# First MLP group of a streaming encoder layer: blocks 0 and 1 go down by seven quadrant products, ahead of the third block's down, with input sums on VectorE and norm transposes placed later

## The chip, the cores and the metric

The kernel runs on one core of a Trainium2 chip. The core has TensorE (matrix products, into PSUM), VectorE, ScalarE and GpSimd (elementwise work; only the first two reach PSUM) and SyncE, which issues transfers; GpSimd issues transfers as well. Each engine takes its own instructions in order and waits on semaphores for the others. The profile calls them PE, DVE, ACT, POOL and SP.

The metric is the device time of one launch in microseconds. Before the change it is 1217.69 us, the median of three runs (1216.7 to 1219.08).

## The reference

The reference computes one layer of a post-norm encoder for 1024 prompt tokens and 32 tokens of a running stream, both of width 1024:

- h = LN(x) * (1 + scale1) + shift1, with the scales, shifts and gates from a conditioning vector;
- a token mixer (gated linear attention in four heads beside a gated MLP with position mixing), an output projection, and x = LN(alpha * x + (1 + gate1) * (mix W_o + b_o));
- h2 = x * (1 + scale2) + shift2, f = relu(h2 W_up + b_up)^2 W_down + b_down, with W_up 1024 x 4096;
- x = LN(alpha * x + (1 + gate2) * f).

All inputs are float32. The kernel splits each factor into a rounded part and a remainder and adds three products (rounded times rounded, and the two mixed ones), so each logical product is three passes on TensorE.

## The kernel before

The 1056 tokens are columns in three blocks: blocks 0 and 1 of 384 prompt tokens, and block 2 of 256 prompt and 32 stream tokens. Activations lie with features on the partitions. The change is in the last stage, which begins with the output projection of blocks 1 and 2 and holds the first norm's second use (norm1), the MLP in eight groups of 512 hidden features, and the last norm.

**Groups 1 to 7.** Blocks 0 and 1 are the two column halves of one matrix, and each group's weights are cut into four quadrants. Up and down are computed for these two blocks by a Strassen-Winograd scheme: seven quadrant products (P1 to P7) in place of eight, with sums of weight quadrants (`_sums`, L1083 to L1086, on GpSimd) and sums of input quadrants. The sums of the up inputs are the same for all groups; `t_prod` (L1260 on) makes them once, from h2 of blocks 0 and 1, in four steps kk: eight sums on GpSimd (L1271 to L1275), then four splits (L1038 on ScalarE, L1039 on VectorE), each written to DRAM (L1281). From there GpSimd loads them into six ring slots (L1323) for each group. For down, `f_split` makes the sums and splits of the hidden activations F from the group itself (L1337 to L1346). The ring slots lie in the memory of h2 of blocks 0 and 1. Block 2 is always computed the plain way (`up_b2`, `down_b2`, L1236 and L1247).

**Group 0.** The first group is plain for all blocks: four up units (L1226, L1227 split the activation) and four down units, each for three blocks. It runs while norm1 of blocks 1 and 2 and `t_prod` are still at work. Its order is: units 0 and 1 on block 0, then on block 1; then a wait for h2 of block 2; then block 2 of units 0 and 1, and units 2 and 3 on all blocks; then a wait for the end of `t_prod`; then the four down units.

**What sets the order.** TensorE's order is written by a planner (`Order`): streams yield planned costs and delays in nanoseconds, and the one of lowest priority number that is due goes next. `yield 0, 2500` in norm1 is such a delay, ahead of the transposes of y (L1142), and the one at L1188 stands ahead of the transposes that make h2 (L227, read out at L233 on VectorE, L236 on ScalarE and L239 on GpSimd). The other engines' order is set by a scheduler that starts from the order of the text.

**Weights.** `W` loads units of 512 KB into four buffers `raw` (SP, L1095) and splits them into eleven buffers `hl` (three more once the ring exists). A split takes one `hl`, and a load one `raw`; `keep` holds some of both back for `t_prod`: a load goes only with more than `keep[0]` buffers free, a split only with more than `keep[1]`. Loads are issued in a fixed order: output projection, group 0's up units, its down units, then the groups.

## Time and profile before

| What | Value |
|---|---|
| Median of three runs | 1217.69 us |
| Profiled execution, its own time | 1219.88 us |
| Span of its profile | 1218.1 us |
| TensorE busy | 1169.3 us, 96% |
| VectorE, ScalarE, GpSimd busy | 75%, 43%, 39% |
| Last output projection's end to group 1's first products | 483.66 to 632.44 us of the span |
| One steady group | about 83.8 us |

All starts are in microseconds from the start of the span. A group of instructions is named by line, engine, operation, and "out<-in" by the program's names; after the bar stand its busy time, the mean length of one in nanoseconds, and the idle time of the engine ahead of it with what ended it. In a timeline each row is a start, a length and a count, with the idle time before in brackets. In a table of windows each engine's column is its busy time, PEclk the granted clock of TensorE as a share of full speed. The chain of waits goes back from the last instruction: at each step to what released it.

### The profile page before, as it was taken

How to read it: one execution, taken by the hardware profiler on the slowest of the kernel's cores; microseconds unless marked ns; L12 is line 12 of the kernel's file. 1: busy time of each engine (PE TensorE's matmuls, PEld its weight loads, DVE VectorE, ACT ScalarE, POOL GpSimd, SP SyncE). 2: the span in 40 equal slices, each digit the busy share in tenths (PEclk: the TensorE clock that was granted, in tenths of full speed). 3: DMA queues.
4: the chain of work that ended last, by engine and by line, in shares of the span. 5: the costliest groups of instructions: out<-in, count | busy, mean ns of one | idle time of the engine just before them, and what ended most of it. 6: DMA issues, size and time to landing. Idle time of an engine off the chain costs nothing.

```text
span 1218.1 us, 22199 instructions
## 1 busy us (share of the span) xinstructions
PE 1169.3 (96%) x8539; PEld 1114.4 (91%) x8539; DVE 909.8 (75%) x1905; ACT 521.2 (43%) x1065; POOL 469.4 (39%) x682
## 2 busy tenths in 40 slices
PE   5999999999899999899989999999999999999996
PEld 3678999988788999799989999999999999999996
DVE  5664797579896688756759769589499597697577
ACT  4462322446566665642425343343443443433321
POOL 2443110345684154348541442334414414422034
PEclk9999999999899999889989999999999999999998
DMA  9632564110012765204762672743825726737412
GB/s 370 239 126 90 180 214 125 36 36 20 23 37 76 263 219 165 83 31 169 251 242 70 210 252 91 244 171 120 300 100 184 265 70 207 246 100 226 157 73 104
DMA packets 49498, 188.46 MB, mean 155 GB/s; under 512 B 5328, under 2 KB 10928, under 8 KB 49392
## 3 DMA queue, kind: packets, MB, share of 16 engines
q1 hardware_dynamic: 31824, 97.38, 23.4%
q0 software_dynamic: 17568, 89.66, 21.5%
q8 instruction: 67, 1.10, 0.4%
q14 instruction: 39, 0.32, 0.1%
HBM read 171.36 MB, written 15.66 MB: 154 GB/s over the span
## 4 chain that ended last, share of the span: by engine, by line
PE 76%; DVE 11%; DMA 4%; POOL 3%; ACT 2%; issue 2%; SPq 0%; POOLq 0%; DVEq 0%; ACTq 0%
PE mm L250 26%; PE mm L1375 16%; PE mm L1442 12%; PE mm L1236 9%; PE mm L284 3%; PE zp L284 3%; DVE hl L1039 2%; DMA raw<-in_w_dram 2%; DVE acc L1467 1%; DMA wst<-in_w_dram 1%; PE zp L250 1%; DMA tdT<-hl 1%; PE mm L1142 1%; PE gt L783 1%; PE mm L227 1%
## 5 line engine op out<-in xcount | busy, mean ns | idle before, releaser
L1038 ACT CAST hl<-raw 128x512 fp32r<-128x512 f32 (+1 forms) x238 | 143.7, 613 | 242.9 <-PE mm L1442 93.3
L1039 DVE TENSOR_TENSOR hl<-raw,hl 128x512 fp32r<-128x512 f32 (+1 forms) x238 | 203.5, 861 | 40.8 <-ACT hl L1038 40.8
L1375 PE MATMUL mm<-ring,hl 128*128 128x384 f32 x960 | 173.7, 338 | 3.4 <-DMA ring<-tdT 3.4
L1375 PEld LDWEIGHTS mm<-ring,hl 128*128 128x128 f32 x960 | 168.9, 190 | 3.8 <-issue 3.7
L1442 PE MATMUL mm<-ring,hl 128*128 128x384 f32 x792 | 140.8, 335 | 1.3 <-DVE acc L1467 1.3
L1442 PEld LDWEIGHTS mm<-ring,hl 128*128 128x128 f32 x792 | 137.5, 188 | 1.9 <-ACT ring L1038 1.4
L250 PE MATMUL mm<-hT,whl 128*128 128x384 f32 (+1 forms) x792 | 129.0, 322 | 0.0
L250 PEld LDWEIGHTS mm<-hT,whl 128*128 128x128 f32 x792 | 127.0, 188 | 1.1 <-issue 1.1
L250 PE MATMUL mm<-h,hl 128*128 128x288 f32 (+1 forms) x756 | 122.3, 318 | 1.7 <-POOL h L239 1.4
L250 PEld LDWEIGHTS mm<-h,hl 128*128 128x128 f32 x756 | 115.4, 196 | 4.6 <-POOL h L239 3.6
L1083 POOL TENSOR_TENSOR raw<-raw 128x512 f32<-128x512 f32 x26 | 35.9, 1383 | 184.7 <-DMA raw<-in_w_dram 155.3
L1467 DVE SCALAR_TENSOR_TENSOR acc<-mm,G,acc 128x384 f32<-128x384 f32 x162 | 93.7, 607 | 5.4 <-PE mm L1442 4.8
L1236 PE MATMUL mm<-fb,hl 128*128 128x288 f32 x708 | 97.0, 295 | 0.0
L1236 PEld LDWEIGHTS mm<-fb,hl 128*128 128x128 f32 x708 | 95.4, 188 | 0.0
L1247 DVE SCALAR_TENSOR_TENSOR acc<-mm,G,acc 128x256 f32<-128x256 f32 (+3 forms) x176 | 61.8, 390 | 12.0 <-PE mm L1236 11.8
L250 PE MATMUL mm<-mhl,hl 128*128 128x384 f32 (+1 forms) x384 | 65.3, 325 | 2.0 <-ACT hl L1038 1.8
L250 PEld LDWEIGHTS mm<-mhl,hl 128*128 128x128 f32 x384 | 60.3, 192 | 2.6 <-ACT hl L1038 2.1
L1323 POOL DMA_DIRECT2D ring<-tdT x56 | 31.3, 560 | 71.8 <-PE mm L1375 38.2
L284 PE MATMUL zp<-zvw,hT 128*128 128x512 f32 x192 | 52.9, 418 | 4.5 <-ACT hT L236 4.5
L1399 DVE TENSOR_TENSOR tmps<-mm,tmps 128x384 f32<-128x384 f32 x28 | 15.6, 558 | 50.4 <-PE mm L1375 50.4
L1345 ACT CAST ring<-F 128x768 fp32r<-128x768 f32 x42 | 35.1, 837 | 40.0 <-DVE F L1337 20.0
L217 POOL TENSOR_SCALAR rs<-mv 128x1 f32<-128x1 f32 (+1 forms) x27 | 8.6, 322 | 111.1 <-DVE mv L216 108.5
(253 smaller groups left out, 2282.2 us busy)
## 6 DMA issues: line engine op xcount, KB each, us to landing
ring<-tdT POOLq DMA_DIRECT2D x56, 768.0 KB, 5.9
raw<-in_w_dram SPq DMA_DIRECT2D x80, 512.0 KB, 3.9
ring<-tdB POOLq DMA_DIRECT2D x42, 768.0 KB, 6.4
wst<-in_w_dram SPq DMA_DIRECT2D x34, 512.0 KB, 4.4
wad<-in_w_dram POOLq DMA_DIRECT2D x24, 512.0 KB, 4.6
tdT<-hl SPq DMA_DIRECT2D x16, 384.0 KB, 2.9
st<-in_w_dram SPq DMA_DIRECT2D x10, 512.0 KB, 10.2
tdB<-h SPq DMA_DIRECT2D x6, 768.0 KB, 4.4
```

What stands on the lines that cost most here:

```text
L250: PE.matmul(pt[:, :n], h[:, a, 128 * kk:128 * kk + 128], act[:, b_, k, :n], start=(i == 0 and j == 0), stop=(i == 7 and j == 2))
L284: PE.matmul(pt[:n, :width], act[:, a, k, off:off + n], hl[:, b_, width * kk:width * kk + width], start=(k == 0 and a + b_ == 0), stop=(k = ...
L1038: S.copy(hl[:, 0, :n], src)
L1039: V.tensor_tensor(hl[:, 1, :n], src, hl[:, 0, :n].bitcast(F32), ALU.subtract)
L1083: G.tensor_tensor(s, a21, a22, ALU.add)
L1236: PE.matmul(pt[:, :n], hl[kk // 2][:, a, o_:o_ + 128], f(kk)[:, c_], start=(kk == 0 and j == 0), stop=(kk == 3 and j == 2))
L1247: V.scalar_tensor_tensor(ac, pt[:, o + lo - p0:o + hi - p0], G2[:, m, c:c + 1], ac, ALU.mult, ALU.add)
L1323: G.dma_start(s, td[t, j].rearrange("p (a c) -> p a c", a=2))))
L1345: S.copy(q[:, 0], src)
L1375: PE.matmul(pt[:, :384], hl[:, a, o_:o_ + 128], quad(ts[j])[:, b_, kk], start=first and j + kk + i == 0, stop=j + kk + i == 4, skip_group_ ...
L1442: PE.matmul(pt[:, :384], hl[:, a, o_:o_ + 128], f[:, b_, kk], start=first and kk + i == 0, stop=kk + i == 3, skip_group_check=True)
L1467: V.scalar_tensor_tensor(ac, v, G2[:, m, 0:1], ac, ALU.mult, ALU.add)
```

## The change

- Group 0's down weights become a bundle with quadrant sums like those of the later groups, and are loaded only after `t_prod` has taken its two `raw` buffers (`W.open`); `keep` now holds back only `hl`.
- `t_prod` takes its two `raw` buffers once and keeps them for all four steps, its sums move from GpSimd to VectorE, its planned step is 7000 instead of 9000, and its priority is ahead of the main stream.
- Group 0's up runs units 0 and 1 on blocks 0 and 1, then units 2 and 3 on blocks 0 and 1, and block 2 of all four units last. For blocks 0 and 1 the activation stays in float32 (`up_plain`: two ScalarE operations), to be split later by `f_split`.
- Group 0's down for blocks 0 and 1 is by seven quadrant products, ahead of block 2's down. The ring's queue starts with group 0's seven splits of F.
- In norm1 the transposes of y are planned 2500 ns later, and those that make h2 of block 2 another 1500.
- The sums kept for P1 start with group 0 instead of group 1.

```diff
@@ -1044,7 +1044,7 @@
...
         self.loads, self.steps, self.out, self.raw = [], [], {}, {}
-        self.keep = (0, 0)
+        self.keep, self.open = 0, False

@@ -1089,14 +1089,14 @@
...
             go = False
-            if self.loads and len(raws.free) > self.keep[0]:
+            if self.loads and raws.free and (self.open or self.loads[0][0][0] != "d"):
                 key, u = self.loads.pop(0)
...
                 slot, f, k = self.steps[0]
-                if (k is None or k in self.raw) and (len(hls.free) > self.keep[1] if slot else halves.free):
+                if (k is None or k in self.raw) and (len(hls.free) > self.keep if slot else halves.free):
                     self.steps.pop(0)
@@ -1122,11 +1122,10 @@
...
     W.unit(("u", 0, m), U_UP + m)
-for i in range(4):
-    W.unit(("d", 0, i), U_DN + i)
-for g in range(1, 8):
+for g in range(8):
     u, d = U_UP + 4 * g, U_DN + 4 * g
-    W.bundle((("u", g, 0), (u, u + 2)), (("u", g, 1), (u + 1, u + 3)))
+    if g:
+        W.bundle((("u", g, 0), (u, u + 2)), (("u", g, 1), (u + 1, u + 3)))
     if g < 7:
@@ -1172,7 +1171,7 @@
...
     tl = xr[b]
-    yield 0, 2500
+    yield 0, 5000
     for wi, (off, n, _) in enumerate(WIN[b]):
@@ -1185,7 +1184,7 @@
...
             x_rows(b + 1)
-    yield 0, 5500 if b < 2 else 2500
+    yield 0, 5500 if b < 2 else 4000
     h2b = actp.tile([P, 2, KT, BLK[b][1]], F32R, tag=f"act{b}", name=f"h2{b}")
@@ -1228,6 +1227,14 @@
...

+def up_plain(hl, m, b, f):
+
+    def done(pt):
+        t = tmp_tile("rl")
+        S.activation(t, pt[:, :384], AF.Relu, bias=col("b_up", m))
+        S.activation(f, t, AF.Square)
+    yield from fm_tile(hl, h2[b], 384, done)
+
 def down_mm(pt, hl, q, f, n):
@@ -1263,16 +1270,18 @@
...
             DM.dma_start(tv[t, j], h2[b][:, :, k0 + 2 * j:k0 + 2 * j + 2, :].bitcast(F32))
+    yield lambda: len(raws.free) >= 2
+    r = [raws.take() for _ in range(2)]
+    W.open = True
     for kk in range(4):
-        yield lambda: len(raws.free) >= 2 and len(hls.free) >= 2
-        r = [raws.take() for _ in range(2)]
+        yield lambda: len(hls.free) >= 2
         b11, b12, b21, b22 = (r[i][:, 512 * j:512 * j + 384] for i in range(2) for j in range(2))
         for d_, b, k in ((b11, 0, kk), (b12, 1, kk), (b21, 0, kk + 4), (b22, 1, kk + 4)):
-            G.tensor_tensor(d_, h2[b][:, 0, k].bitcast(F32), h2[b][:, 1, k].bitcast(F32), ALU.add)
-        G.tensor_tensor(b11, b12, b11, ALU.subtract)
-        G.tensor_tensor(b12, b22, b12, ALU.subtract)
-        G.tensor_tensor(b22, b22, b11, ALU.subtract)
-        G.tensor_tensor(b21, b21, b22, ALU.subtract)
+            V.tensor_tensor(d_, h2[b][:, 0, k].bitcast(F32), h2[b][:, 1, k].bitcast(F32), ALU.add)
+        V.tensor_tensor(b11, b12, b11, ALU.subtract)
+        V.tensor_tensor(b12, b22, b12, ALU.subtract)
+        V.tensor_tensor(b22, b22, b11, ALU.subtract)
+        V.tensor_tensor(b21, b21, b22, ALU.subtract)
         for t, src in (("T1", b11), ("T3", b12), ("T2", b22), ("T4", b21)):
@@ -1280,10 +1289,10 @@
...
             hls.give(h)
-        for x_ in r:
-            raws.give(x_)
-        yield 0, 9000
-    W.keep = (0, 0)
+        yield 0, 7000
+    for x_ in r:
+        raws.give(x_)
+    W.keep = 0

@@ -1317,7 +1326,7 @@
...
     def queue(self):
-        for _, _, t, _, _ in SEQ:
+        for _, _, t, _, _ in SEQ if self.g else ():
             for j in range(2):
@@ -1420,12 +1429,14 @@
...
                 yield 12 * cost(288), 0
-        W.done("d", g, r, "A21")
+        for a_ in ("A21",) if g else ("A11", "A12", "A21", "A22"):
+            W.done("d", g, r, a_)

...
         g = self.g
-        for r in range(2):
-            yield from self.down_b2(r)
+        if g:
+            for r in range(2):
+                yield from self.down_b2(r)
         self.sums = [{}, {}, {}]
@@ -1444,8 +1455,12 @@
...
                     yield 6 * cost(384), 0
-                W.done("d", g, r, a_)
+                if g or a_[0] == "S":
+                    W.done("d", g, r, a_)
             ring.done("f", g, t)
+        if not g:
+            for r in range(2):
+                yield from self.down_b2(r)

@@ -1454,7 +1469,7 @@
...
         if prod == "P1":
-            if self.g == 1:
+            if self.g == 0:
                 S.copy(p1[m], v)
@@ -1557,51 +1572,40 @@
...

-    W.keep = (2, 3)
+    W.keep = 3
     yield lambda: h2[0] is not None
-    tp = order.add(t_prod(), 7)
-    f_a = [pd.tile([P, 2, 2, 768], F32R, tag="F", name="f", bufs=1)]
-
-    def fa(m, b):
-        return f_a[m // 2][:, m % 2, :, 384 * b:384 * b + 384]
-    hl = [W.unit_of("u", 0, m) for m in range(2)]
-    for m in range(2):
-        yield from up_std(hl[m], m, 0, fa(m, 0))
-    yield lambda: h2[1] is not None
-    f_a.append(pd.tile([P, 2, 2, 768], F32R, tag="R", name="f", bufs=2))
-    for m in range(2):
-        yield from up_std(hl[m], m, 1, fa(m, 1))
+    tp = order.add(t_prod(), 5)
+    groups = [Group(g) for g in range(8)]
+    g0 = groups[0]
+    g0.f = pd.tile([P, 4, 768], F32, tag="F", name="F", bufs=1)
+    hl = []
+
+    def up_first(ms, b):
+        yield lambda: h2[b] is not None
+        for m in ms:
+            while len(hl) <= m:
+                hl.append(W.unit_of("u", 0, len(hl)))
+            yield from up_plain(hl[m], m, b, g0.f[:, m, 384 * b:384 * b + 384])
+    for ms, b in (((0, 1), 0), ((0, 1), 1), ((2, 3), 0), ((2, 3), 1)):
+        yield from up_first(ms, b)
+    tmps_t = pd.tile([P, 8, 384], F32, tag="R", name="tmps", bufs=2)
+    tmps = Slots([tmps_t[:, i] for i in range(6)])
+    p1 = [tmps_t[:, 6], tmps_t[:, 7], pd.tile([P, 384], F32, name="p1")]
     yield lambda: h2[2] is not None
...
     for m in range(4):
-        if m > 1:
-            hl.append(W.unit_of("u", 0, m))
-            for b in range(2):
-                yield from up_std(hl[m], m, b, fa(m, b))
         yield from up_std(hl[m], m, 2, fb2[:, m])
         W.unit_done("u", 0, m)
+    g0.have |= {"C11", "C12", "C21", "C22"}
     yield lambda: tp not in order.streams
...
                  .rearrange("p (a n) -> p a n", a=2) for i in range(3)]
-    groups = [Group(g) for g in range(8)]
-    for gr in groups[1:]:
+    for gr in groups:
         gr.queue()
     ring.pump()
-    for i in range(4):
-        hl = W.unit_of("d", 0, i)
-        for b in range(3):
-            for q in range(2):
-                pt = mm()
-                n = BLK[b][1]
-                down_mm(pt, hl, q, lambda kk: fb2[:, kk] if b == 2 else fa(kk, b), n)
-                down_ev(pt, 4 * (i % 2) + 2 * (i // 2) + q, ((b, 0, n),))
-                yield 12 * cost(n), 0
-        W.unit_done("d", 0, i)
-    tmps_t = pd.tile([P, 8, 384], F32, tag="R", name="tmps", bufs=2)
-    tmps = Slots([tmps_t[:, i] for i in range(6)])
-    p1 = [tmps_t[:, 6], tmps_t[:, 7], pd.tile([P, 384], F32, name="p1")]
+    yield from g0.down()
     for g in range(1, 7):
```

## The prediction

> **What bounds the kernel now.** I read the page first (shares, chain of waits by line), then a table of windows over the stretch that the change touches, then the TensorE timeline in it, then the chain of waits ahead of each gap.
>
> ```profile
> span 1218.1 us, 22199 instructions
> PE 1169.3 (96%) x8539; PEld 1114.4 (91%) x8539; DVE 909.8 (75%) x1905; ACT 521.2 (43%) x1065; POOL 469.4 (39%) x682
> PE 76%; DVE 11%; DMA 4%; POOL 3%; ACT 2%; issue 2%; SPq 0%; POOLq 0%; DVEq 0%; ACTq 0%
> ```
>
> TensorE is busy for 96% of the span and makes 76% of the chain that ended last. An edit is worth what it takes off TensorE's own work and off its gaps. The gaps near the change, by windows (first column from:to, then the length, then each engine's busy time; PEclk is the granted clock):
>
> ```profile
> core 0: us, PE busy (x) PEld busy (x) DVE busy (x) ACT busy (x) POOL busy (x), PEclk, DMA share, GB/s
> 483.66:632.44 148.78, 138.05 (x791) 132.47 (x790) 95.09 (x162) 63.60 (x123) 80.09 (x81) 0.91 0.45 161
> 483.66:497.00 13.34, 7.75 (x41) 7.24 (x40) 9.06 (x16) 7.20 (x14) 5.70 (x7) 0.74 0.44 145
> 497.00:509.86 12.86, 12.86 (x82) 12.66 (x79) 10.01 (x21) 8.02 (x12) 4.57 (x8) 1.00 0.32 124
> 509.86:530.40 20.54, 18.82 (x77) 14.28 (x76) 12.62 (x31) 13.54 (x33) 10.13 (x12) 0.67 0.07 26
> ...
> 621.90:632.44 10.54, 7.12 (x26) 6.84 (x25) 3.83 (x5) 2.05 (x3) 5.96 (x8) 0.68 1.03 383
> 660.00:690.00 30.00, 30.00 (x177) 30.00 (x176) 27.31 (x49) 10.79 (x18) 13.24 (x13) 1.00 0.53 170
> ```
>
> The TensorE timeline (start, length, line, shape, count, idle time before and its releaser) gives the prices and the gaps:
>
> ```profile
> 490.26 0.48 PE L1142 MATMUL mm<-ident,y 128*128 128x128 f32 x1 [5.59 <-ACT y L952]
> ...
> 496.62 1.04 PE L1142 MATMUL mm<-ident,y 128*128 128x128 f32 x8
> 497.41 4.45 PE L250 MATMUL mm<-h,hl 128*128 128x384 f32 x24
> ...
> 509.86 4.35 PE L227 MATMUL mm<-ident,xr 128*128 128x128 f32 x24
> 514.14 0.67 PE L250 MATMUL mm<-h,hl 128*128 128x288 f32 x3
> ...
> 587.40 8.52 PE L1236 MATMUL mm<-f,hl 128*128 128x384 f32 x48
> 595.76 3.36 PE L1236 MATMUL mm<-fb,hl 128*128 128x288 f32 x24
> 598.96 4.95 PE L250 MATMUL mm<-h,hl 128*128 128x288 f32 x36
> ...
> 625.58 7.03 PE L1375 MATMUL mm<-ring,hl 128*128 128x384 f32 x24 [3.42 <-DMA ring<-tdT]
> ```
>
> From start to start, 48 products of 384 columns take 8.36 us (0.174 each), 24 of 288 columns 3.20 us (0.133 each), eight transposes 0.79 us (0.1 each). With these I price what each window held and call the rest lost:
> - Gap A, 483.66 to 497.00: 18 products of 384 and 22 transposes are 5.3 us of work in 13.3, so 8 us lost: 5.59 us of standing still, then half clock (PEclk 0.74 on average).
> - Gap B, 509.86 to 530.40: 24 transposes and 53 products of 288 are 9.5 us in 20.5, so 11 us lost. The third block's input arrives row by row through VectorE, ScalarE and GpSimd, and the clock is at 0.67.
> - Gap C, 621.90 to 632.44: 24 products of 384 are 4.2 us in 10.5, so 6.2 us lost.
>
> What lies behind A and C, from the chain of waits in order of time:
>
> ```profile
> 482.16 6.43 DMA raw<-in_w_dram
> ...
> 488.61 1.14 ACT hl L1038 x2
> 489.75 0.47 ACT y L952
> ...
> 611.42 8.02 DMA raw<-in_w_dram
> ...
> 619.62 0.09 POOL raw L1083
> ...
> 620.85 4.59 DMA ring<-tdT
> ```
>
> In A, ScalarE stood at the cast of a weight half whose load landed late; the eviction of y that the transposes need was queued behind it. In C, GpSimd stood at a weight sum waiting for its load, and the ring's load was issued behind it.
>
> **The change part by part.** It removes 24 products of TensorE: down for blocks 0 and 1 was 4 units x 2 blocks x 24 = 192 products of 384 columns and becomes 7 x 24 = 168. 24 x 0.174 = **4.2 us gained**; the third block's 96 products only move behind them. Nothing on another engine can take this back unless it makes TensorE wait, so that is costed below.
>
> Gap A: the gate on loads keeps the down units' four loads off SP's queue until the input sums have their buffers, so their casts leave ScalarE's queue here, and the transposes of y come 2.5 us of planned time later, behind ready products. Bounds 0 (another cast takes that place) and 8; I take **6 gained**, since both parts work against the same wait.
>
> Gap B: units 2 and 3 on blocks 0 and 1 (96 products, 16.7 us) now stand ahead of the third block. The norm chain also starts 2.5 us later and gets a further 1.5 us before its second transposes, and shares VectorE with the input sums, so I leave some wait at the third block. Bounds 0 and 11; **7.5 gained**.
>
> Gap C: the ring's loads for group 1 are issued while the third block's 12.8 us of down products run, a longer cover than the 3.42 us that were idle, though they now queue on POOL behind seven splits' slots and eight weight sums. Bounds 0 and 6.2; **5 gained**.
>
> What is added lands mostly on VectorE. Its rows in 483.66 to 632.44, then in a steady group (857.30 to 941.06), and two single instructions:
>
> ```profile
> L1039 DVE TENSOR_TENSOR hl<-raw,hl 128x384 fp32r<-128x384 f32 x16 | 12.5, 784 | 11.6 <-ACT hl L1038 11.6
> L1247 DVE SCALAR_TENSOR_TENSOR acc<-mm,G,acc 128x384 f32<-128x384 f32 x16 | 9.6, 610 | 1.3 <-PE mm L1236 1.3
> L1227 DVE TENSOR_TENSOR f<-rl,f 128x384 fp32r<-128x384 f32 x8 | 5.3, 656 | 1.7 <-ACT f L1226 1.6
> L1225 DVE TENSOR_TENSOR rl<-rl 128x384 f32<-128x384 f32 x8 | 5.0, 626 | 6.6 <-ACT rl L1221 6.6
> ```
>
> ```profile
> L1039 DVE TENSOR_TENSOR hl<-raw,hl 128x512 fp32r<-128x512 f32 x26 | 20.7, 796 | 2.4 <-ACT hl L1038 2.4
> L1467 DVE SCALAR_TENSOR_TENSOR acc<-mm,G,acc 128x384 f32<-128x384 f32 x27 | 15.6, 607 | 0.8 <-PE mm L1442 0.7
> L1346 DVE TENSOR_TENSOR ring<-F,ring 128x768 fp32r<-128x768 f32 x7 | 6.6, 950 | 0.6 <-ACT ring L1345 0.6
> L1337 DVE TENSOR_TENSOR F<-F 128x768 f32<-128x768 f32 x1 | 1.5, 1472 | 0.0
> L1340 DVE TENSOR_TENSOR F<-F 128x768 f32<-128x768 f32 x1 | 0.9, 950 | 0.0
> ```
>
> ```profile
> 538.92 0.56 DVE L1225 TENSOR_TENSOR rl<-rl 128x384 f32<-128x384 f32 x1 [2.46 <-ACT rl L1221]
> ...
> 541.50 1.27 DVE L1039 TENSOR_TENSOR hl<-raw,hl 128x384 fp32r<-128x384 f32 x1 [0.23 <-ACT hl L1038]
> ```
>
> ```profile
> raw<-in_w_dram SPq DMA_DIRECT2D x80, 512.0 KB, 3.9
> L1083 POOL TENSOR_TENSOR raw<-raw 128x512 f32<-128x512 f32 x26 | 35.9, 1383 | 184.7 <-DMA raw<-in_w_dram 155.3
> ```
>
> VectorE gains 32 input sums (0.56 each: 17.9 us), seven splits of F (6.6), four differences of F (4.3), eight splits of weight sums (8 x 0.8: 6.4) and 27 - 16 = 11 adds (6.7); it loses the square and the remainder of eight up tiles (5.3 + 5.0). Net 31.6 us: 95 becomes 127 us, in a stretch that would be 149 - 29 = 120 us if every gap closed. So **VectorE takes over part of the gain**, at two places.
>
> Start of the quadrant products. From 483.66 TensorE has 15.7 tiles' worth: 180 products of 384 (31.3 us), some 63 transposes (6.3) and 96 of 288 (12.8), so it would arrive at 534, or 537 with the 3.5 us left in gap B. The first product needs the F quadrant split into ring slots that lie in the old inputs, so all input sums must be read out first. VectorE by then: 9.06 + 10.01 + 12.62 = 31.7 us that it did up to 530.4, less 4.5 for eight up-tile operations, plus 48 input operations at 0.56 (26.9), plus one split (0.95): 55 us, so 539. The second half of that product needs a unit whose buffer the sums hold: 538 + 3.9 for its load + about 1.5 to split = 543.5, against 541. Behind it on TensorE stands everything. 1.6 + 2.4 and about 1 at a lower clock: **5 lost**; bounds 0 (sums spread evenly under the up products) and 12 (VectorE at the 0.78 of the contended row: 48 x 0.22 = 10.6 more, part of it under the wait left in B).
>
> Pace of the quadrant products. 168 x 0.174 = 29.2 us of TensorE; VectorE has 15.6 of adds, six splits and four differences of F (10.0), twelve weight splits (9.6): 35.2. The first product's sums stay in PSUM until they are read, so VectorE's lateness becomes TensorE's: **6 lost**. Lower bound 0: 660 to 690 shows 27.3 us of VectorE in 30 without a TensorE gap, and the third block's products behind can absorb later work. Upper bound 12: the third product waits for the seventh of eight weight sums, 7 x 1.38 = 9.7 us against 8.4 of cover, and the other 512-wide splits rise as in contended rows.
>
> ScalarE's additions (seven F casts, eight weight casts; a square for a copy) fit its 64 us in 149. SP issues as many loads and input writes as before. GpSimd loses 32 sums and gets eight of 1.38.
>
> Sum: -4.2 - 6 - 7.5 - 5 + 5 + 6 = **-11.7 us** on the profiled execution's 1219.88 (span 1218.1), so 1208.2; the median of the runs shown, 1217.69, lies 2.2 lower, so **1206**.
>
> The port shows in the two single rows: 0.56 us alone, 1.27 beside a GpSimd operation. The Trainium skill, GPSIMD Engine Reference, Specifications, has GpSimd share its SBUF interfaces with VectorE and contend with VectorE instructions of two SBUF inputs; the trace agrees. By that rule the moved sums shed the GpSimd operations that blocked VectorE, but each can still be held by the 16 GpSimd remainders of the norms, and if half of them meet one, 8 x 0.71 us later at the first product leaves a sum of -6.0.
>
> At 621.90 to 632.44 a wait of 3.42 us is followed by a mean clock of 0.68. The Trainium skill, TensorE: Matmul & The Clock Gate, part 1, lets one idle window of about 3.4 us halve the clock; that speaks against the change, as a wait of 4 us at the first quadrant product would then cost some 2.7 more (the 24 products of that window took 6.9 us for 4.2): -9 in all, 1209.
>
> **The rivals.**
> - Full cover: VectorE works ahead. Gains 4.2 + 8 + 9.5 + 6, losses 2 + 1: -24.7, so 1193. For it: VectorE stands idle for 54 of the 149 us before. Against: its 127 us of work.
> - Eaten by VectorE: gap B gains only 4, the two losses are 8 and 10: -1.2, so 1216.5. For it: the same 127 us.
> - The change doesn't do what it says: another cast holds ScalarE in gap A, and the later transposes only delay the third block: A 0, B 4, rest as forecast, -2.2, so 1215.5. For it: ScalarE's order is the scheduler's, not the text's.
> - Slower: VectorE runs at contended prices through the group. The input part then ends 10.6 us later, so 16 at the first product and 3 at half clock (19); quadrant products 16 late (twelve weight splits and ten F operations half as dear again, 10 more); B 0. -4.2 - 6 - 0 - 5 + 19 + 16 = +19.8, so 1237. It decides from the point where VectorE's lateness passes the 22.7 us of the four gains. For it: 0.78 instead of 0.56 in the row of 16. Against: GpSimd's 32 sums, which made that row, are gone.
>
> **How the numbers follow.** Forecast 0.45 (its own range 1199 to 1213), full cover 0.17, eaten 0.12, not doing what it says 0.08, slower 0.18. Measurement tells 0.2% (2.4 us) from no change. Faster: 0.45 + 0.17 + half of the two small cases = 0.72; same: their other half, 0.10; slower 0.18. The range is 1194 to 1221: a little of full cover and most of slower lie outside.
>
> **What would show it.** Right: no wait for y at ScalarE after the last output projection; 168 products of line 1442's kind ahead of 96 of the third block's in the first group; no ring wait at group 1's first products; VectorE near 9 tenths from the norms to group 1. Wrong: a wait of over 8 us at the first F product, TensorE idle inside the seven products, or a granted clock of 0.5 twice there. A trace with the gaps closed and the time unchanged would put the loss into group 1 or later, which I expect unchanged.

## The result and the profile after

The changed kernel took **1212.63 us** (median of five runs, 1210.38 to 1212.73) beside 1218.76 us of the kernel before on the same chip: a ratio of 0.9946, 95% interval 0.9933 to 0.9960, so 0.54% sooner; the two medians lie 6.1 us apart. The forecast was 1206, with the range 1194 to 1221. The profiled execution took 1212.71 us, against 1219.88 before. Of the executions below, one of the kernel with the weight sums on VectorE took 1779.78 us at a granted clock of 0.592 and is left out there: its median is 1211.20 us, and 1211.88, which a later expectation quotes, counts it in.

The page of the kernel after, its span, TensorE's row and the shares of the chain that ended last:

```profile
span 1210.9 us, 22196 instructions
PE 1161.5 (96%) x8515; PEld 1106.3 (91%) x8515; DVE 929.3 (77%) x1954; ACT 529.7 (44%) x1080; POOL 455.1 (38%) x658
PE 75%; DVE 13%; issue 3%; DMA 3%; POOL 3%; ACT 2%; SPq 0%; DVEq 0%; ACTq 0%; POOLq 0%
```

TensorE has 24 instructions fewer (8515 for 8539), as the change intends. VectorE has 19.5 us more of busy time and 13% of the chain where it had 11%. The TensorE timeline of the kernel after shows where the time stands (L250 up, L227 transposes, L1453 the quadrant products of down, L1243 the third block's down):

```profile
488.47 1.30 PE L250 MATMUL mm<-h,hl 128*128 128x384 f32 x6 [2.46 <-DVE acc L1198]
...
512.21 0.24 PE L227 MATMUL mm<-ident,xr 32*128 32x32 f32 x1 [2.37 <-ACT xr L1182]
...
546.80 4.33 PE L1453 MATMUL mm<-ring,hl 128*128 128x384 f32 x24
555.12 4.86 PE L1453 MATMUL mm<-ring,hl 128*128 128x384 f32 x18 [3.99 <-ACT tmps L1473]
561.54 5.47 PE L1453 MATMUL mm<-ring,hl 128*128 128x384 f32 x30 [1.57 <-DVE acc L1482]
568.06 2.36 PE L1453 MATMUL mm<-ring,hl 128*128 128x384 f32 x12 [1.05 <-DVE acc L1482]
...
584.82 12.35 PE L1243 MATMUL mm<-fb,hl 128*128 128x288 f32 x92
...
597.54 1.75 PE L250 MATMUL mm<-h,hl 128*128 128x288 f32 x12
...
681.34 6.55 PE L250 MATMUL mm<-h,hl 128*128 128x288 f32 x48
```

The same place in the kernel before, the start of group 2's up:

```profile
689.04 6.15 PE L250 MATMUL mm<-h,hl 128*128 128x288 f32 x45
```

Group 2 starts 7.7 us sooner (681.34 for 689.04) and the span is 7.2 us shorter: the gain is made in the first group and at the start of the second, and then kept. Group 1 itself starts only 1.4 us sooner (597.54 for 598.96).

The table of windows of the kernel after, from the up stage to group 1's first products, and two stretches inside it (the third number from the end is the granted clock):

```profile
483.66:546.80 63.14, 56.78 (x327) 52.81 (x326) 58.45 (x115) 44.66 (x89) 27.87 (x25) 0.92 0.40 144
546.80:584.82 38.02, 31.41 (x170) 30.46 (x169) 33.72 (x50) 11.58 (x21) 23.10 (x16) 0.96 0.47 155
584.82:597.54 12.72, 12.72 (x97) 12.72 (x97) 11.47 (x25) 4.98 (x8) 5.11 (x4) 1.00 0.34 104
597.54:628.90 31.36, 31.36 (x194) 31.36 (x193) 16.14 (x26) 13.40 (x24) 12.64 (x15) 1.00 0.75 258
514.00:520.80 6.80, 6.80 (x22) 5.78 (x22) 6.80 (x18) 4.09 (x11) 3.19 (x3) 0.50 0.51 182
555.00:558.40 3.40, 3.28 (x10) 3.28 (x11) 3.40 (x3) 2.14 (x6) 3.32 (x3) 0.51 0.42 154
```

The third number after the length is VectorE: 58.45 of 63.14 us, then 33.72 of 38.02, then 11.47 of 12.72. From the norms to group 1 it is busy for 103.6 of 113.9 us (0.91). The first of these three stretches, up to the first quadrant product, is called the up stage from here on. By the trace it holds 173 products of 384 columns, 96 of 288 and 57 transposes, at the prediction's prices 30.1 + 12.8 + 5.7 = 48.6 us of TensorE work. (The prediction's 50.4 us are for 180 products and some 63 transposes; the trace before has 59 transposes. In the trace after, TensorE had done 21 of the 192 products of 384 columns by 483.66, and before only 12.) So the up stage loses 63.1 - 48.6 = **14.5 us**, and the quadrant products 38.0 - 29.2 = **8.8 us**. Group 1's first stretch runs without a stop; before, it held gap C. The last two rows are stretches at half clock, one behind the stop of 2.37 us, one behind that of 3.99.

The longest stop among the quadrant products has this history (timeline of the kernel after, GpSimd, ScalarE and VectorE; L1084 and L1085 are weight sums, L1038 casts of weight halves, L1473 the eviction of the first product, L1355, L1351 and L1349 the work on F):

```profile
544.39 8.30 POOL L1084 TENSOR_TENSOR raw<-raw,raw 128x512 f32<-128x512 f32 x1 [3.94 <-DVE hl L1039]
545.47 0.95 DVE L1351 TENSOR_TENSOR F<-F 128x768 f32<-128x768 f32 x1
548.15 0.94 DVE L1349 TENSOR_TENSOR F<-F 128x768 f32<-128x768 f32 x1
...
550.62 0.95 DVE L1355 TENSOR_TENSOR ring<-F,ring 128x768 fp32r<-128x768 f32 x1
552.72 0.62 ACT L1038 CAST hl<-raw 128x512 fp32r<-128x512 f32 x1 [5.43 <-POOL raw L1084]
552.77 1.27 POOL L1085 TENSOR_TENSOR raw<-raw,raw 128x512 f32<-128x512 f32 x1
...
554.07 0.62 ACT L1038 CAST hl<-raw 128x512 fp32r<-128x512 f32 x1 [0.73 <-POOL raw L1085]
554.59 0.85 ACT L1473 COPY tmps<-mm 128x384 f32<-128x384 f32 x2
```

While VectorE worked without a break, one GpSimd sum took 8.30 us; it ended at 552.69, 1.1 us after the last VectorE instruction shown, and the next sum took 1.27. Two casts on ScalarE waited for GpSimd, and the evictions of the first product (the copies of its sums out of PSUM), which were ready, stood behind them. TensorE stood for 3.99 us.

### The profile page after: what moved, and what is told of

Read it like the earlier page. It is cut to its first block, busy times and chain, and to the rows that moved or that the text cites. A ratio compares the mean times of both kernels' runs of the same rounds, so it can differ in the third digit from the quotient of the medians.

```text
span 1210.9 us, 22196 instructions
## 1 busy us (share of the span) xinstructions
PE 1161.5 (96%) x8515; PEld 1106.3 (91%) x8515; DVE 929.3 (77%) x1954; ACT 529.7 (44%) x1080; POOL 455.1 (38%) x658
## 4 chain that ended last, share of the span: by engine, by line
PE 75%; DVE 13%; issue 3%; DMA 3%; POOL 3%; ACT 2%; SPq 0%; DVEq 0%; ACTq 0%; POOLq 0%
PE mm L250 20%; PE mm L1384 16%; PE mm L1453 14%; PE mm L1243 11%; PE zp L284 3%; PE mm L284 3%; DVE hl L1039 2%; DMA raw<-in_w_dram 1%; DVE acc L1482 1%; DMA wst<-in_w_dram 1%; DVE t L233 1%; PE zp L250 1%; DVE bst L208 1%; PE gt L783 1%; PE mm L472 1%
## 5 line engine op out<-in xcount | busy, mean ns | idle before, releaser
L1038 ACT CAST hl<-raw 128x512 fp32r<-128x512 f32 (+1 forms) x236 | 143.0, 614 | 227.8 <-PE mm L1453 104.6
L1039 DVE TENSOR_TENSOR hl<-raw,hl 128x512 fp32r<-128x512 f32 (+1 forms) x236 | 190.6, 813 | 25.2 <-ACT hl L1038 24.8
L1453 PE MATMUL mm<-ring,hl 128*128 128x384 f32 x924 | 165.9, 337 | 6.6 <-ACT tmps L1473 4.0
L1453 PEld LDWEIGHTS mm<-ring,hl 128*128 128x128 f32 x924 | 161.7, 189 | 7.6 <-ACT tmps L1473 4.3
L1384 PE MATMUL mm<-ring,hl 128*128 128x384 f32 x900 | 161.1, 334 | 0.6 <-DMA ring<-tdT 0.6
L1384 PEld LDWEIGHTS mm<-ring,hl 128*128 128x128 f32 x900 | 156.0, 188 | 1.1 <-DMA ring<-tdT 1.1
L250 PE MATMUL mm<-h,hl 128*128 128x288 f32 (+1 forms) x852 | 132.2, 311 | 3.5 <-DVE acc L1198 2.5
L250 PEld LDWEIGHTS mm<-h,hl 128*128 128x128 f32 x852 | 125.2, 192 | 4.8 <-issue 2.7
L250 PE MATMUL mm<-hT,whl 128*128 128x384 f32 (+1 forms) x792 | 129.0, 322 | 0.0
L250 PEld LDWEIGHTS mm<-hT,whl 128*128 128x128 f32 x792 | 127.0, 188 | 1.1 <-issue 1.1
L1482 DVE SCALAR_TENSOR_TENSOR acc<-mm,G,acc 128x384 f32<-128x384 f32 x189 | 109.4, 606 | 6.5 <-PE mm L1453 5.7
L1243 PE MATMUL mm<-fb,hl 128*128 128x288 f32 x576 | 81.1, 295 | 0.0
L1243 PEld LDWEIGHTS mm<-fb,hl 128*128 128x128 f32 x576 | 78.2, 188 | 0.0
L250 PE MATMUL mm<-mhl,hl 128*128 128x384 f32 (+1 forms) x384 | 63.3, 319 | 2.0 <-ACT hl L1038 1.8
L1038 ACT CAST ring<-raw 128x512 fp32r<-128x512 f32 x52 | 32.4, 622 | 66.8 <-PE mm L1453 36.2
L250 PEld LDWEIGHTS mm<-mhl,hl 128*128 128x128 f32 x384 | 58.7, 188 | 2.6 <-ACT hl L1038 2.1
L1084 POOL TENSOR_TENSOR raw<-raw,raw 128x512 f32<-128x512 f32 x28 | 45.1, 1611 | 40.2 <-DVE hl L1039 34.6
L1254 DVE SCALAR_TENSOR_TENSOR acc<-mm,G,acc 128x256 f32<-128x256 f32 (+2 forms) x160 | 52.2, 365 | 9.6 <-PE mm L1243 9.6
## 6 DMA issues: line engine op xcount, KB each, us to landing
st<-in_w_dram SPq DMA_DIRECT2D x10, 512.0 KB, 10.2
```

Of the source, the lines that this page charges most:

```text
L250: PE.matmul(pt[:, :n], h[:, a, 128 * kk:128 * kk + 128], act[:, b_, k, :n], start=(i == 0 and j == 0), stop=(i == 7 and j == 2))
L1038: S.copy(hl[:, 0, :n], src)
L1039: V.tensor_tensor(hl[:, 1, :n], src, hl[:, 0, :n].bitcast(F32), ALU.subtract)
L1084: G.tensor_tensor(a21, a11, a21, ALU.subtract)
L1243: PE.matmul(pt[:, :n], hl[kk // 2][:, a, o_:o_ + 128], f(kk)[:, c_], start=(kk == 0 and j == 0), stop=(kk == 3 and j == 2))
L1254: V.scalar_tensor_tensor(ac, pt[:, o + lo - p0:o + hi - p0], G2[:, m, c:c + 1], ac, ALU.mult, ALU.add)
```

## The experiments

Each kernel was timed beside the kernel before, which lay at 1218.2 to 1219.0 us; two changed kernels are compared by their ratios to it, and a difference of ratios is turned into us with 1218.7. The columns on the right of this table are read off each kernel's trace (us): the TensorE timeline, and VectorE's busy time in the window of the seven products. Each trace is one execution, and places in it differ by some us for reasons that the edit doesn't give: by 483.66 TensorE had done 0 to 24 of the 192 products of 384 columns, and the profiled execution of "weight sums held" is the fastest of its six, those of "norm delays back" and "later turns" the slowest of theirs.

```
kernel                     ratio to before [95%]    first quadrant  seven    VectorE  start of
                                                    product at      take     in them  group 1's up
changed kernel             0.9946 [0.9933, 0.9960]  546.8           38.0     33.7     597.5
weight sums held           0.9941 [0.9925, 0.9956]  542.3           39.4     36.5     594.4
input sums on GpSimd       0.9963 [0.9950, 0.9975]  549.4           36.9     32.4     599.0
norm delays back           0.9967 [0.9954, 0.9980]  551.4           39.6     34.4     603.7
order only                 0.9974 [0.9961, 0.9988]  none            -        -        588.4
weight sums on VectorE     0.9932 [0.9916, 0.9947]  545.3           39.1     33.5     597.1
third block's down first   0.9994 [0.9982, 1.0007]  574.0           29.2     25.2     603.2
no input sums              0.9896 [0.9882, 0.9910]  543.8           34.3     30.1     590.9
later turns                0.9941 [0.9925, 0.9957]  549.1           38.6     33.8     600.5
shift to ScalarE           0.9925 [0.9906, 0.9943]  546.6           35.8     32.6     595.1
shift + sums on VectorE    0.9882 [0.9865, 0.9899]  544.8           34.5     32.1     592.0
  and later turns          0.9882 [0.9863, 0.9902]  545.6           30.1     26.8     588.4
no quadrant products       0.9913 [0.9897, 0.9929]  none            -        -        587.2
```

The time of the seven goes with VectorE's work that falls inside them: with 26.8 us or less of it they take at most 0.9 us more than their price of 29.2. The table alone does not say which is the cause, since a longer stretch also takes in more of VectorE's work.

My first theory was **ScalarE's queue**: the evictions stand behind casts that wait for GpSimd's sums. The rival was **VectorE's amount of work**: whichever instruction is named, TensorE follows VectorE, which is full.

**Weight sums held.** The splits of group 0's weight sums are not put into the queues until the first product is evicted.

```diff
-                    self.keep, self.open = 0, False
+                    self.keep, self.open, self.hold = 0, False, True
...
-                        if self.steps:
+                        if self.steps and not (self.hold and self.steps[0][2] is None):
...
+                        if prod == "P1":
+                            W.hold = False
```

> The changed kernel, with the splits of group 0's sums of down weights put in the text only after the first quadrant product's evictions. Theory, ScalarE's queue: in the changed kernel the copies of the first product (line 1473) stand behind two casts of weight sums that wait for GpSimd (an idle ScalarE of 5.43 us, then TensorE's 3.99 us gap and half clock). With the casts behind the copies the 3.99 us gap and most of the slow clock go: the seven products take about 32 us instead of 38.0, and the time is 6 us less, about 1206.5. Rival, VectorE sets the pace of the seven products: the wait moves to the adds of line 1482, and no more than 2 us are gained, about 1211.

Measured 1211.51 us, by the ratios 0.05% below the changed kernel, with intervals that overlap almost wholly. Its TensorE timeline, and a row of ScalarE's:

```profile
552.14 2.29 PE L1453 MATMUL mm<-ring,hl 128*128 128x384 f32 x6 [3.04 <-ACT p L1475]
558.18 9.13 PE L1453 MATMUL mm<-ring,hl 128*128 128x384 f32 x42 [3.76 <-DVE acc L1484]
```

```profile
550.36 0.83 ACT L1354 CAST ring<-F 128x768 fp32r<-128x768 f32 x1 [3.32 <-DVE F L1349]
```

No weight cast ahead of the evictions waits for GpSimd any more, yet 6.8 us of stops stand in the same stretch, 3.76 of them ended by VectorE, and the seven products take 39.4 us. The other 3.04 us end with an eviction that again stood behind a cast on ScalarE, now one of F, which waited 3.32 us for VectorE. So the weight casts are not what costs the time; that ScalarE's order plays a part is not ruled out.

**Input sums on GpSimd**, as before the change.

```diff
-                        V.tensor_tensor(d_, h2[b][:, 0, k].bitcast(F32), h2[b][:, 1, k].bitcast(F32), ALU.add)
-                    V.tensor_tensor(b11, b12, b11, ALU.subtract)
...
+                        G.tensor_tensor(d_, h2[b][:, 0, k].bitcast(F32), h2[b][:, 1, k].bitcast(F32), ALU.add)
+                    G.tensor_tensor(b11, b12, b11, ALU.subtract)
```

> The changed kernel, with the 32 input sums back on GpSimd and everything else as changed. Theory, VectorE is full in the up phase (13.31 of 13.34, 12.46 of 12.46, 23.19 of 25.74 us) and that is what delays the norms there: the up phase, 63.1 us from 483.66 to the first quadrant product, gets 4 to 8 us shorter in its gaps, but 32 sums of 1.15 us beside the norms' remainders on GpSimd end some 10 us later than on VectorE, so the first quadrant product waits: in all 0 to +6 us, 1212 to 1219. Rival, the sums on VectorE cost nothing there: the up phase keeps its gaps and the later sums add to them, +8 us or more, above 1220.

Measured 1214.71 us, 0.17% above the changed kernel, with intervals that overlap a little. The first quadrant product comes 2.6 us later, and the seven lose 7.7 us instead of 8.8. VectorE may be the better place for these sums, by about 2 us, but the intervals do not quite tell that from nothing. In the up stage VectorE has 51.4 us of work here for 58.5, and GpSimd 57.2 for 27.9: VectorE's lighter load brought nothing, because the sums came later.

**Norm delays back** to 2500 and 2500.

```diff
-                yield 0, 5000
+                yield 0, 2500
...
-                yield 0, 5500 if b < 2 else 4000
+                yield 0, 5500 if b < 2 else 2500
```

> The changed kernel, with the norms' planned delays back at 2500. Theory, the later transposes cover waits: without them TensorE reaches the transposes before VectorE and ScalarE have their inputs, the gaps before 497 and at 510 grow, +4 us, about 1216.5. Rival, the delays do nothing because the chain through VectorE sets when the inputs are there: within 1.5 us of 1212.6.

Measured 1215.31 us, 0.21% above the changed kernel, again with intervals that touch. The first quadrant product comes 4.6 us later in its trace, an execution 2.8 us above that kernel's median. The delays are worth about 2.6 us.

**Order only.** The kernel before, with units 2 and 3 on blocks 0 and 1 ahead of the third block's up.

```diff
+                hl += [W.unit_of("u", 0, m) for m in range(2, 4)]
+                for b in range(2):
+                    for m in range(2, 4):
+                        yield from up_std(hl[m], m, b, fa(m, b))
...
-                    if m > 1:
-                        hl.append(W.unit_of("u", 0, m))
-                        for b in range(2):
-                            yield from up_std(hl[m], m, b, fa(m, b))
```

> The kernel before, with one edit: group 0's up units 2 and 3 on blocks 0 and 1 stand ahead of the third block's up. Down stays plain, the input sums stay on GpSimd, the delays stay. Theory, the order alone hides the third block's wait (gap B, 11 us lost): 2 to 3 us of it are left, so 8 us are gained, about 1210.5 beside 1218.8, with gaps A and C as before. Rival, the third block's chain or the input sums then end later by as much, and less than 3 us are gained, above 1215.5.

Measured 1214.72 us, between the two. Its TensorE timeline:

```profile
488.16 0.47 PE L1142 MATMUL mm<-ident,y 128*128 128x128 f32 x1 [5.08 <-ACT y L952]
...
603.16 6.20 PE L1375 MATMUL mm<-ring,hl 128*128 128x384 f32 x34 [2.12 <-DVE hl L1039]
...
615.25 1.54 PE L1375 MATMUL mm<-ring,hl 128*128 128x384 f32 x6 [3.81 <-DMA ring<-tdT]
```

Gap A's wait for y stays, gap B is gone (group 1's up starts at 588.4 where it started at 598.96), and more than half of that is given back in group 1's first products, to VectorE's splits and the ring's loads. The new order by itself brings group 1 forward by 10.5 us, more than the 7.5 that the prediction gave gap B; what follows group 0 takes most of it away, and 0.26% (3.2 us) reaches the end.

**Weight sums on VectorE.** Group 0's eight down weight sums move from GpSimd.

```diff
-                    G.tensor_tensor(s, a21, a22, ALU.add)
-                    G.tensor_tensor(a21, a11, a21, ALU.subtract)
+                    E = V if key[:2] == ("d", 0) else G
+                    E.tensor_tensor(s, a21, a22, ALU.add)
+                    E.tensor_tensor(a21, a11, a21, ALU.subtract)
...
```

> The changed kernel with the eight weight sums of the first group's down matrices (four per pair of units) on VectorE, where GpSimd made them; in the changed kernel's trace GpSimd's took 30.2 us in 483.66 to 584.82, one of them 8.30 us while VectorE worked back to back, and TensorE's first long stop among the quadrant products (3.99 us) lay behind two casts that waited for it. Theory (the slow GpSimd sum costs the stop): the 3.99 us and the 3.4 us of half clock behind it go, about -4 us, 1208.5 us. Rival (VectorE's work is what TensorE follows, whoever is named): eight sums of about 0.7 us more on VectorE, +3 us or more, 1215 us or above. Between 1211 and 1214 the two cancel.

Measured 1211.20 us, by the ratios 0.14% below the changed kernel with intervals that overlap: no difference that this can tell. (In the changed kernel's trace the eight sums took 19.2 us on GpSimd, not 30.2.) The 8.30 us sum is gone, but three stops of 1.74, 2.58 and 3.16 us stand in its place, two of them ended by VectorE.

**Third block's down first**, as in the other groups, with the weight buffers given back in the order that goes with it.

```diff
-                    if g:
-                        for r in range(2):
-                            yield from self.down_b2(r)
+                    for r in range(2):
+                        yield from self.down_b2(r)
...
-                    if not g:
-                        for r in range(2):
-                            yield from self.down_b2(r)
...
```

> The changed kernel with the first group's plain down products of the third block ahead of its seven quadrant products, as in the other groups. Theory (at 546.80 VectorE is behind, and the quadrant products are stopped by that): the plain products, 12.7 us of TensorE with light evictions, give VectorE time for the splits of the weights and of F, and the stops of 8.8 us in the quadrant products shrink to 3 or less; -5.5 us, 1207 us. Rival (the quadrant products' own evictions and splits are more than VectorE can keep pace with, wherever they stand): the stops stay or move to the second group's up, 1211 to 1215 us.

Measured 1217.81 us, which is no faster than the kernel before: this order takes back the whole gain. Its timeline, TensorE and then VectorE:

```profile
545.08 0.29 PE L1243 MATMUL mm<-fb,hl 128*128 128x288 f32 x1
555.36 1.57 PE L1243 MATMUL mm<-fb,hl 128*128 128x288 f32 x5 [9.98 <-DVE fb L1226]
560.10 0.61 PE L1243 MATMUL mm<-fb,hl 128*128 128x288 f32 x1 [3.18 <-ACT fb L1225]
...
574.02 14.75 PE L1452 MATMUL mm<-ring,hl 128*128 128x384 f32 x84
...
603.17 3.08 PE L250 MATMUL mm<-h,hl 128*128 128x288 f32 x22
```

```profile
545.09 2.02 DVE L1351 TENSOR_TENSOR F<-F 128x768 f32<-128x768 f32 x1
...
550.98 2.01 DVE L1349 TENSOR_TENSOR F<-F 128x768 f32<-128x768 f32 x1
552.91 2.02 DVE L1355 TENSOR_TENSOR ring<-F,ring 128x768 fp32r<-128x768 f32 x1
554.86 0.81 DVE L1226 TENSOR_TENSOR fb<-rl,fb 128x288 fp32r<-128x288 f32 x2
```

The stops left the seven products, as the theory has it, but a larger one came ahead of them. The seven products run from 574.02 to 603.17 without a stop, 29.2 us, the prediction's price: **the products are not slow; in the changed kernel the engines that serve them, VectorE above all, were behind**. But TensorE stood for 13.2 us ahead of them, waiting for the third block's split activations, which in VectorE's order came behind the work on F. The place "behind" that the change gives the third block's products hides that wait. I had expected 1207.

**No input sums.** The 32 sums are left out: T1 to T4 are split from unsummed inputs, so the later groups' results differ from the reference's.

```diff
-                        V.tensor_tensor(d_, h2[b][:, 0, k].bitcast(F32), h2[b][:, 1, k].bitcast(F32), ALU.add)
-                    V.tensor_tensor(b11, b12, b11, ALU.subtract)
...
+                    b11, b12, b21, b22 = (h2[i][:, 0, kk + 4 * j].bitcast(F32) for j in range(2) for i in range(2))
```

> The changed kernel without the 32 input sums (the four sum operands T1 to T4 are split from unsummed parts of the inputs, so the later groups' results are other than the reference's): 19.3 us of VectorE work gone from 483.66 to 546.80, in which VectorE is busy for 58.5 of 63.1 us and TensorE has 47.9 us of work. Theory (gaps A and B come back as new stops because VectorE is full there): TensorE reaches the first quadrant product at 537 to 540 rather than 546.8, and as little of that is lost behind it, the end comes 5 to 8 us sooner, 1205 to 1208 us. Rival (the stops are ScalarE's queue order and the half clock behind a wait, not VectorE's amount of work): less than 3 us, 1210 us or above.

Measured 1206.32 us, ratio 0.9896: by the ratios 6.1 us (0.50%) below the changed kernel, as the theory of VectorE's amount has it. Its trace, the seven products' start and end, and its windows:

```profile
543.79 7.66 PE L1448 MATMUL mm<-ring,hl 128*128 128x384 f32 x42
554.71 9.01 PE L1448 MATMUL mm<-ring,hl 128*128 128x384 f32 x42 [3.27 <-DVE acc L1477]
...
578.13 12.88 PE L1243 MATMUL mm<-fb,hl 128*128 128x288 f32 x96
```

```profile
483.66:546.80 63.14, 57.14 (x339) 52.48 (x338) 48.09 (x86) 46.69 (x95) 29.01 (x29) 0.97 0.36 132
```

The place is not the expected one. The first quadrant product comes only 3.0 us sooner, at 543.8 and not at 537 to 540, though VectorE is down to 48.09 of 63.14 us; 3.7 us are gained inside the seven products. So the input sums explain less than a third of the 14.5 us lost in the up stage. What holds the rest is not settled; the stops that remain there are short ones, 1.12 us at most, for the halves of the inputs (L236 on ScalarE, L239 on GpSimd) and for the starts of the accumulator (L1195 on ScalarE, L1198 on VectorE). Without the sums the splits also have one step less to wait for, so this run does not part VectorE's amount of work from the length of that chain.

**Later turns.** The third block's transposes back to channels 4 us later in the plan.

```diff
-                yield 0, 5500 if b < 2 else 4000
+                yield 0, 5500 if b < 2 else 8000
```

> The changed kernel with the third block's transposes back to channels started 4 us later in the plan (8000 for 4000), behind more of the first two blocks' up. Theory (TensorE is at these transposes before ScalarE has normalised the rows: 2.37 us of waiting, and half clock for 6.9 us behind it, worth 3.4): about -4 us in the up stage; of that, what VectorE's amount of work doesn't hold back, -2 to -5 us at the end, 1208 to 1210.5 us. Rival (VectorE's work sets the end of the up stage): the wait moves to the third block's up, 1211.5 to 1214 us.

Measured 1212.13 us: no difference. The 2.37 us stop at 512 went, and stops of 1.31 and 2.21 us came at the third block's up. That is the rival.

**Shift to ScalarE.** The accumulator's start for all channels, and the squares of the third block's up.

```diff
-                        if k % 2:
+                        if True:
                             S.activation(accb[:, k, off:off + w], pt[:, off:off + w], AF.Identity,
...
-                    if ring:
+                    if True:
                         S.activation(t[:, :n], t[:, :n], AF.Square)
```

> The changed kernel with two kinds of VectorE work put on ScalarE: the even channels' start of the accumulator from the transposed tiles (11 instructions, 5.0 us in 483.66 to 546.80) and the squares of the third block's up (four of 0.44 us). Theory (the amount of VectorE work in 483 to 585 sets the pace of TensorE; without the input sums, 19.3 us of it, the end came 6.3 us sooner, so about a third of what is taken off comes back): 6.8 us off VectorE give -2.2 us, 1210 us. Rival (ScalarE's queue, 44.7 us busy of 63.1 there, becomes the one that TensorE waits for): 1212 us or above.

Measured 1209.72 us, 0.21% below the changed kernel, the size that was expected, with intervals that touch. The seven products take 35.8 us.

**Shift and weight sums on VectorE together**: the last edit and the one on weight sums.

```diff
-                    G.tensor_tensor(s, a21, a22, ALU.add)
+                    E = V if key[:2] == ("d", 0) else G
+                    E.tensor_tensor(s, a21, a22, ALU.add)
...
-                        if k % 2:
+                        if True:
...
```

> The kernel before this one in the list (accumulator start and third block's squares on ScalarE), and with it the first group's down weight sums on VectorE instead of GpSimd, as in the earlier run that had them alone (1211.88 us against 1212.63). Theory (VectorE's room decides, and GpSimd beside a busy VectorE is slow): the 6.8 us freed take in the 5 us of the sums, and GpSimd's 8.30 us sum is gone from the chain: 1208 to 1210 us. Rival (each VectorE microsecond costs the same, whatever it does): 5 us back on, 1212 us.

Measured **1205.02 us**, ratio 0.9882: below the expected band, and by the ratios 7.8 us (0.64%) below the changed kernel, where the two edits alone gave 1.7 and 2.6 (0.14% and 0.21%). The seven products take 34.5 us. Together they give more than the sum of the two, by 0.29%; the four intervals taken together leave about 0.3% of doubt on that, so it is suggested and not shown. It fits the earlier run, in which the slow GpSimd sum was gone and a full VectorE gave the stops other names.

**And later turns**: the same with the edit that made no difference alone.

```diff
-                yield 0, 5500 if b < 2 else 4000
+                yield 0, 5500 if b < 2 else 8000
```

> The kernel with the accumulator start and the third block's squares on ScalarE and the weight sums on VectorE (1205.02 us), and with the third block's transposes 4 us later in the plan (8000 for 4000), which made no difference to the changed kernel alone (1212.13 against 1212.63). In the trace of the 1205.02 us kernel TensorE stands 4.63 us at these transposes and then runs 6.9 us at half clock, 8 us lost in all. Theory (a stop can be taken away once VectorE has room behind it): at least 3 of the 8 us come back, 1199 to 1202 us. Rival (VectorE is still what sets the end of the up stage, 56.2 busy of 63.1 us): the wait moves to the third block's up as it did without these two edits, 1204 to 1206 us.

Measured 1204.13 us, ratio 0.9882, the same as without it: the rival. The trace has moved, though. TensorE's timeline and the window of half clock:

```profile
525.79 0.40 PE L250 MATMUL mm<-h,hl 128*128 128x288 f32 x1 [0.57 <-ACT h L236]
526.89 0.53 PE L250 MATMUL mm<-h,hl 128*128 128x288 f32 x2 [0.70 <-POOL h L239]
528.68 0.61 PE L250 MATMUL mm<-h,hl 128*128 128x288 f32 x1 [1.26 <-ACT h L236]
...
545.63 7.45 PE L1454 MATMUL mm<-ring,hl 128*128 128x384 f32 x42
553.73 7.55 PE L1454 MATMUL mm<-ring,hl 128*128 128x384 f32 x42 [0.66 <-DVE acc L1483]
```

```profile
527.90:538.10 10.20, 7.03 (x25) 6.02 (x26) 8.26 (x15) 8.93 (x22) 3.29 (x3) 0.51 0.33 112
```

The seven products now take 30.1 us, nearly their price, but the up stage ends where it did: the stop went to the third block's input, with 10.2 us at half clock.

**No quadrant products.** The kernel before, with the changed kernel's order of up, delays, input sums on VectorE and plan of `t_prod` (step and priority), and group 0's down in plain products.

```diff
-                yield 0, 2500
+                yield 0, 5000
...
-                yield 0, 5500 if b < 2 else 2500
+                yield 0, 5500 if b < 2 else 4000
...
-                        G.tensor_tensor(d_, h2[b][:, 0, k].bitcast(F32), h2[b][:, 1, k].bitcast(F32), ALU.add)
+                        V.tensor_tensor(d_, h2[b][:, 0, k].bitcast(F32), h2[b][:, 1, k].bitcast(F32), ALU.add)
...
-                    yield 0, 9000
+                    yield 0, 7000
...
-                tp = order.add(t_prod(), 7)
+                tp = order.add(t_prod(), 5)
```

(on top of the kernel with the order only)

> The kernel before with the order of the up stage, the later norm transposes and the input sums on VectorE of the change, but with the first group's down in plain products as before and no quadrant products in it: what the change does without its quadrant products. Theory by the prediction's sum (-4.2 us for 24 fewer products, but 8.8 us of stops in them that the plain products do not have, and the third block's later place that hides the wait for its split inputs): 1211 to 1216 us, at or above the changed kernel. Rival (the quadrant products are a loss here, and the order, the delays and the sums make the gain): 1205 to 1210 us.

Measured 1208.95 us, ratio 0.9913 (0.9897 to 0.9929), below the changed kernel's whole interval: the rival. The gain comes from the order, the delays and the place and plan of the sums; **the quadrant products, with what they bring along (their weight sums, the splits of F, the held-back loads), are a loss here of about 4 us**. How much of the gain each of the other parts makes in this kernel was not tested, nor whether the later edits above would help it too. Its windows, TensorE's timeline and GpSimd's:

```profile
483.66:540.97 57.31, 54.73 (x336) 51.75 (x335) 43.83 (x94) 35.49 (x71) 17.00 (x22) 0.97 0.18 67
540.97:587.18 46.21, 46.21 (x290) 46.21 (x289) 37.23 (x77) 12.84 (x25) 5.91 (x8) 1.00 0.75 263
587.18:625.81 38.63, 34.33 (x195) 32.46 (x194) 27.14 (x34) 16.27 (x30) 22.96 (x21) 0.96 0.62 218
```

```profile
609.22 1.29 PE L1375 MATMUL mm<-ring,hl 128*128 128x384 f32 x6 [2.26 <-DMA ring<-tdT]
```

```profile
600.96 1.11 POOL L1323 DMA_DIRECT2D ring<-tdT  x2
609.86 1.26 POOL L1083 TENSOR_TENSOR raw<-raw 128x512 f32<-128x512 f32 x1 [7.79 <-DMA raw<-in_w_dram]
611.08 1.65 POOL L1323 DMA_DIRECT2D ring<-tdT  x3
```

Without the quadrant products the up stage takes 57.3 us instead of 63.1, with VectorE at 43.83 us in it, and the plain down 46.2 us without a stop, so group 1 starts at 587.2, 10.4 us ahead of the changed kernel, though TensorE had 4.2 us more to do. Gap C is there again (38.6 us for 31.4), but the chain behind its longest stop is another: the 2.26 us ended at 609.22 with a load of the ring, and the last two loads before that had left GpSimd from 600.96 on. GpSimd's wait of 7.79 us for a weight unit, with three of the ring's loads right behind the sum, holds up only what comes after; stops of 0.68, 0.52 and 0.37 us follow. Why the earlier loads landed late is not settled. So the quadrant products' account against this kernel is -4.2 for 24 products, -7.3 for gap C, +8.8 for their own stops and +5.8 for the up stage: +3.1 us in the traces, where the ratios say 0.33%, 4 us.

## Why the prediction was right, and where it was not

The sign and the range held; the forecast was 6.6 us too low, at the upper edge of its own range (1213). About 1.1 of the 6.6 us lies in the base, which is 1217.69 us for three runs and 1218.76 for five. In the profiled executions the sum promised -11.7 and the time moved by -7.2. Term by term:

- **24 fewer products, -4.2.** Right: 8515 instructions for 8539, and 168 products at 0.174 where nothing stops them (third block's down first: 29.2 us). But "nothing on another engine can take this back unless it makes TensorE wait" is just what happened.
- **Gaps A and B and the wait at the first product, -6 - 7.5 + 5 = -8.5.** In the trace the three make 14.5 us lost where A and B had 19: -4.5. Another 1.6 us (9 products) had come ahead of 483.66, which no term holds and no edit explains: -6.1 in all. The parts were placed wrongly. ScalarE's wait for y went from gap A as said, but a stop of 2.46 us for VectorE's accumulator start took its place; 2.37 us for the third block's rows stayed in B; and the first quadrant product waited for nothing, because TensorE itself came to it at 546.8, where I had it at 534 to 537 and the product's operands at 543.5. The error is that I priced the new waits only at the point where the chains meet, and not along the up stage.
- **Gap C, -5.** It was -6.2: group 1's first stretch takes 31.36 us without a stop. The order alone and the kernel without quadrant products have stops there again, so it is the quadrant products, with what they bring along, that cover it, and not the earlier order.
- **Pace of the quadrant products, +6.** It was 8.8. VectorE's amount was right in size, 33.7 us there against 35.2 forecast. What the sum left out is that lateness is worse than its own length: a GpSimd sum of 8.30 us instead of the 1.38 of the prediction's row, casts behind it, evictions behind these, and 3.4 us at half clock after the 3.99 us stop. The runs with the sums held and with the weight sums on VectorE took the waiting casts and the slow sum away, and the seven still lost 10.2 and 9.9 us, so neither is the cause by itself. VectorE's load is the reading that fits best: without the input sums, 19.3 us less, 6.1 us came back, 3.7 of them here. It is argued more than shown, since that run shortens a chain as well, the run with the sums on GpSimd lightens VectorE and gains nothing, and the gain of the shift to ScalarE alone is within its interval.

These four give -4.2 - 6.1 - 6.2 + 8.8 = -7.7, as the start of group 2 does.

So the steps that were off are the -8.5 for A, B and the wait at the first product, which the up stage gave as -4.5 because new stops took the place of the old ones along it, and the +6 for the pace, which was 8.8. That the total still fell into the forecast's own range is in part luck: gap C gave 1.2 us more than its term, and 1.6 us came from ahead of the stretch. And none of the rivals asked what the rest of the change would do without the quadrant products, the part that the change is named for: it does better by 0.33%.

Of the rivals, "eaten by VectorE" named the mechanism that fits the seven products (8.8 us lost, where it has 10), and the time lies between it and the forecast. "The change doesn't do what it says" fell: y's wait is gone. In the order alone it stays (5.08 us). With the gate on loads and the old delays it is 0.32 us, with the delays and no gate (no quadrant products) it is not there: by these two traces either part removes it, or nearly. "Slower" fell: the wait at the first product was 0, not 16 to 19. Of the marks that I named as wrong, TensorE idle inside the seven products is there.

The sentence on SBUF interfaces gave -6.0 by the rule of the Trainium skill, GPSIMD Engine Reference, Specifications. The span moved by -7.2, nearer to that than to my sum, but by another way: VectorE was not held at the first product, GpSimd was starved behind it. The sum with a clock cost behind a wait at the first quadrant product, -9, had the wrong place too: that wait was 0, and the half clock of 3.4 us came behind the 3.99 us stop inside the products.

One step was costed at nothing ("only move behind them") and hid a condition, though it is not what the forecast missed by: the place of the third block's products. Put ahead of the seven they wait 13.2 us, and the whole gain is gone.

## What to carry to other kernels

Cutting the bottleneck engine's work by an algebraic scheme need not pay where the engines that feed it are nearly full in that very stage: 24 products saved 4.2 us and brought VectorE to 0.91 of a stretch, and the same kernel without them was 4 us faster. So run the rest of a change without the part that it is named for. When a stop moves under another name each time that its named cause is taken away, try to take work off the fullest engine instead of working on the name, and try together the edits that bring little alone: two that could hardly be told from nothing gave 7.8 us together. Ask of every reorder what the new place covers: with the products that were "only moved" put first, TensorE waited 13 us.

## What the runs showed of the hardware

- **Contention of VectorE and GpSimd can fall on either side.** In the changed kernel a 128x512 GpSimd sum took 8.30 us while VectorE's instructions beside it took their normal 0.95 us. With the third block's down first, the same VectorE instructions took 2.0 us, while GpSimd sums such as this one stood beside them:

```profile
544.43 1.86 POOL L1085 TENSOR_TENSOR raw<-raw,raw 128x512 f32<-128x512 f32 x1
```

  The Trainium skill, GPSIMD Engine Reference, Specifications, has the two share SBUF interfaces; the traces agree, and show that a price for one engine is not enough.
- **Half clock came without a long stop.** In the kernel with the shift, the sums on VectorE and later turns no stop from 484 to 527.9 us was over 1.3 us; by its timeline TensorE stood for 1.75 of the 3.4 us before (0.57, 0.70 and the first 0.48 of 1.26), and 10.2 us at a granted clock of 0.51 followed, with more stops in them. In the changed kernel a stop of 2.37 us was followed by 6.8 us at 0.50. The Trainium skill, TensorE: Matmul & The Clock Gate, Part 1, lets one idle window of about 3.4 us bring it; by these rows less than that can be enough. It is not always: in the kernel with the weight sums on VectorE a stop of 2.65 us, ended at 489.09, was followed by a granted clock of 1.00 up to 511 us.
